# P times v channel-major with v stationary on the two column halves, a normalised P, channel-major gates and an ordered start, in a four-layer hybrid attention kernel

## The chip, the cores and the metric

The kernel runs on one core of a Trainium2 chip. The metric is the device time of one execution in microseconds; a kernel is timed in several runs and the median counts. PE is TensorE, DVE VectorE, ACT ScalarE, POOL GpSimd, SP the queue of SyncE.

## The reference, cut to what matters

There are 256 tokens of 1024 channels, all in fp32. Two "first" layers have three mixers side by side (mLSTM, MoBA with 4 heads, NSA with 4 heads), an output projection and a feed-forward part. Two "second" layers have differential (4 heads), stick-breaking (8 heads) and forgetting attention (8 heads), of which each output is multiplied by a SiLU gate.

```python
def first_block(x, ...):
    for l in range(DEPTH):
        h = rmsnorm(x, norm_mix[l])
        proj = jnp.einsum('bsd,de->bse', h, w_in[l])
        ...                                   # split into m_*, b_*, n_*
        y_m = mlstm(qk[..., :M_WIDTH], qk[..., M_WIDTH:], m_v, m_o, ...)
        y_b = moba(b_q, b_k, b_v, ...)        # here: causal softmax over 256
        y_n = nsa(n_q, n_kc, n_vc, n_ks, n_vs, n_kw, n_vw, n_g, ...)
        mix = jnp.concatenate([y_m, y_b, y_n], axis=-1)
        x = x + jnp.einsum('bse,ed->bsd', mix, w_out[l])
        h = rmsnorm(x, norm_ffn[l])
        u = jnp.square(jax.nn.relu(jnp.einsum('bsd,df->bsf', h, w_ff1[l])))
        x = x + jnp.einsum('bsf,fd->bsd', u, w_ff2[l])
...
# nsa:  gj[:, 0] * o_c + gj[:, 1] * o_s + gj[:, 2] * o_w
def hybrid_layer(x, ...):
    p = rms_norm(x, g_pre) @ w_in
    qa, ka, va, ga, qs, ks, vs, gs, qf, kf, vf, gf, ff = jnp.split(p, split_at, axis=-1)
    ...
    ya = merge(diff_attention(qa, ka, ...)) * jax.nn.silu(ga)
    yb = merge(stick_breaking_attention(qs, ks, vs)) * jax.nn.silu(gs)
    yc = merge(forgetting_attention(qf, kf, vf, cum_log_f)) * jax.nn.silu(gf)
    y = jnp.concatenate([ya, yb, yc], axis=-1) @ w_out
    return x + rms_norm(y, g_post)
```

## The kernel before

**Products with weights.** Each weight unit (for the most part 512 KB) is loaded by SP into one of four raw buffers, and split into a high and a low part in fp32r (`whi` on ACT, line 154; `wlo` on DVE, line 166, and on POOL, line 162, in turns). The activations are split likewise into `xh` and `xl`. A product is three fp32r matmuls (`mm3`, line 262). In `xchunk` the activations are stationary and up to 512 columns of weights move, so the output is token-major (128 tokens x 512 channels). In `wpair` 128 columns of weights are stationary and the 256 tokens move, so the output is channel-major. `rows_all` is the output projection and the second half of the feed-forward part; it takes its left sides from `mix`, channel-major tiles of 256 channels that have been split into `mh` and `ml`, under the keys m, b, n (first layers) and d, s, x (second layers).

**Mixers.** They are written as tasks in two queues ("lanes"), which advance a step at a time between the matmuls of the main stream; a scheduler then sets the order of every engine's instructions. Lane 0 has three PSUM banks, lane 1 two. An attention task of four heads is `att4`: `scores2` makes the scores of two heads at once (64 rows of the array each), DVE masks them, and ACT takes exp with the row sums `den`; `ptr` transposes P in 128 x 128 blocks (line 734); `pv` multiplies a stationary block of the transposed P (128 keys x 128 tokens) by 64 columns of v, three matmuls a head; the token-major output is then multiplied by 1/den on DVE, for NSA by its gates, for s and x by the gates too. `to_mix` transposes it (four per key, line 779) and splits it (ACT line 780, DVE line 781). The diff task scales its P before the transposes (lines 1229, 1230).

**Gates.** Those of s and x come from `xchunk` (token-major, `ev_gate`, line 1385): tanh on ACT, and a DVE instruction at line 1396.

**Start.** SP asks for the first 128 columns of the constants, norm_mix, the four quarters of x with the first weight unit between them, two more units, the other 1568 columns of the constants, and one more unit. POOL's queue asks at once for small rows spread to all partitions (`setup2`, line 370), `cmp_w2`, `diff_lambda` and `m_norm`. Ten bf16 dummy matmuls warm PE (`WARM`); eight transposes of x for each half (`xT`, line 589) come ahead of the first product, of 268 columns.

Of the kernel before, what the change touches and what calls it, by code (L numbers as in the profile page):

```python
# [28 lines left out]
C_CZC = 128  # L29
C_DIF = 512  # L30
C_ML = 896
C_SB = 1152
C_TRI = 1280
C_COS = 1408
C_SIN = 1440
C_CM = 1472
C_CM1 = 1504
C_SUM = 1536
C_KBD = 1552
C_VBD = 1554  # L40
C_S8 = 1558
C_MONE = 1566
C_ONE = 1567
C_DUP = 1568
# [70 lines left out]
class Stream:  # L115
# [16 lines left out]
    def load(self):  # L132
        u = self.n_load
        self.n_load += 1
        a, b, dmas = self.units[u]
        t = self.k.wraw.tile([128, self.SUB], F32, name="raw", tag="raw")
        v = t[:, :a * b].rearrange("p (a b) -> p a b", a=a)
        for f, src in dmas:
            self.k.nc.sync.dma_start(f(v), src)
        self.raw[u] = v, t  # L140
# [42 lines left out]
class K:  # L183
# [132 lines left out]
    def setup(self):  # L316
# [9 lines left out]
        for h in range(2):  # L326
            for tt in range(2):
                sl = slice(h * 512, h * 512 + 512)
                nc.sync.dma_start(self.x[:, tt, sl], A["x"][0, tt * 128:(tt + 1) * 128, sl])
            self.w.load()  # L330
# [15 lines left out]
        self.w.load()  # L346
        nc.sync.dma_start(cp[:, 128:], A["consts"][:, 128:])
        for h in range(2):
            self.bound_half(h, None, False, self.colm, True, "i")
        ps = self.gt()  # L350
        for i in range(self.WARM):
            self.mm(ps, wz[:, :128], wz, True, True)

    def setup2(self):
# [12 lines left out]
        self.rp = {}  # L367
        for name, n in rows:
            self.rp[name] = rp[:, o:o + n].rearrange("p (l c) -> p l c", l=2)
            nc.gpsimd.dma_start(rp[:, o:o + n], dram(A[name], 0, [[0, 128], [1, n]]))  # L370
            o += n
        self.w2 = self.cst.tile([128, 2, 2, 64], F32, name="w2")
        nc.gpsimd.dma_start(self.w2, A["cmp_w2"].rearrange("l w j d -> j l w d"))
# [9 lines left out]
        self.msb = self.cst.tile([128, 128], BF16, name="msb")  # L383
        nc.vector.tensor_copy(self.msb, cp[:, C_SB:C_SB + 128])
        self.s8 = self.cst.tile([128, 8], F32R, name="s8")
        nc.scalar.activation(self.s8, cp[:, C_S8:C_S8 + 8], AF.Copy)
        self.tri = self.cst.tile([128, 129], F32R, name="tri")
        nc.scalar.activation(self.tri[:, 0:128], cp[:, C_TRI:C_TRI + 128], AF.Copy)
        nc.scalar.activation(self.tri[:, 128:129], cp[:, C_MONE:C_MONE + 1], AF.Copy)
# [6 lines left out]
        lt = st[:, 512:1024]  # L396
        nc.gpsimd.dma_start(lt, dram(A["diff_lambda_2"], 0, [[0, 128], [1, 512]]))
        lv = lt.rearrange("p (l a b d) -> p l a b d", l=2, a=2, b=2)
        t = st[:, 1024:1280].rearrange("p (l a d) -> p l a d", l=2, a=2)
# [7 lines left out]
        self.mn = self.cst.tile([128, 512], F32, name="mn")  # L407
# [4 lines left out]
    def plan(self):  # L412
# [41 lines left out]
        for l in range(2):  # L454
# [6 lines left out]
            xch(t, l, W, 3584, 512)  # L461
            xch(t, l, W, 5632, 520)
            for c in range(4096, 5120, 256):
                cols(t, l, W, c, 256, 4)
            xch(t, l, W, 5120, 512)
# [115 lines left out]
    def xT(self, lane, kts, tts, gcol):  # L581
# [5 lines left out]
        for a, kt in enumerate(kts):  # L587
            for b, tt in enumerate(tts):
                i = nc.tensor.transpose(ps[:, a * w + b * 128:a * w + (b + 1) * 128], self.x[:, tt, kt * 128:(kt + 1) * 128],  # L589
                                        self.ident)  # L590
                if nt == 1:
                    self.order(i, "blocks")
# [17 lines left out]
    def bound_half(self, h, acc, scaled, gcol, bcast, flag):  # L610
# [10 lines left out]
        for q in range(2):  # L621
            self.xT(self.lanes[q], (h * 4 + 2 * q, h * 4 + 2 * q + 1), (0, 1), gcol)
# [60 lines left out]
    def ffn(self, l, hold, bound):  # L683
# [17 lines left out]
        def items():  # L701
            m = ff1(0)
            for b in range(16):
# [42 lines left out]
    def att4(self, lane, qf, kf, vf, scale, mask=C_CZC, extra=None, vwait=None):  # L746
# [3 lines left out]
        den = lane.sb("den", 8, bufs=2).rearrange("p (h t) -> p h t", h=4)  # L750
        for h in (0, 2):
            self.scores2(lane, P, nmx, den, h, [(qf(i), kf(i), extra(i) if extra else None) for i in (h, h + 1)], mask, scale)
            yield
# [118 lines left out]
    def nsa_task(self, lane, l, nsA, nq):  # L872
# [48 lines left out]
        o = lane.w().rearrange("p (t h d) -> p t h d", t=2, h=4)  # L921
        for w in range(2):
            ps, rd = yield from self.att4(
                lane, lambda h: qrT[(h % 2) * 64:(h % 2) * 64 + 64, h // 2],
                lambda h: kT[(h % 2) * 64:(h % 2) * 64 + 64, w],
                lambda h, st: nsA[:, st, w * 128 + 64:w * 128 + 128], 0.125)
            gr = lane.sb("gr", 8).rearrange("p (t h) -> p t h", t=2)
            nc.vector.tensor_tensor(gr, gt[:, :, 4 + 4 * w:8 + 4 * w], rd.rearrange("p h t -> p t h"), ALU.mult)
            if w == 0:
                for tt in range(2):  # L930
                    nc.vector.tensor_tensor(o[:, tt], ps[:, tt], gr[:, tt, :, None].to_broadcast([128, 4, 64]), ALU.mult)
            else:
                o2 = lane.w().rearrange("p (t h d) -> p t h d", t=2, h=4)
                for tt in range(2):
                    nc.vector.tensor_tensor(o2[:, tt], ps[:, tt], gr[:, tt, :, None].to_broadcast([128, 4, 64]), ALU.mult)
                nc.gpsimd.tensor_tensor(o, o, o2, ALU.add)
            yield
# [27 lines left out]
        ps = lane.ps()  # L965
        for tt in range(2):
            self.mm(ps[:, tt * 256:(tt + 1) * 256], pc[:64, tt * 128:(tt + 1) * 128],
                    self.vbd.rearrange("p h d -> p (h d)"), True, True)
        o = o.rearrange("p t h d -> p t (h d)")
        nc.vector.tensor_tensor(o, ps.rearrange("p (t c) -> p t c", t=2), o, ALU.add)  # L970
        yield
        yield from self.to_mix(lane, o, ["n%d" % l])

    def moba_task(self, lane, l, qk, bv):
# [29 lines left out]
        ps, rd = yield from self.att4(  # L1004
# [3 lines left out]
        o = lane.w().rearrange("p (t h d) -> p t h d", t=2, h=4)  # L1008
        for tt in range(2):
            nc.vector.tensor_tensor(o[:, tt], ps[:, tt], rd[:, :, tt, None].to_broadcast([128, 4, 64]), ALU.mult)  # L1010
        yield
        yield from self.to_mix(lane, o.rearrange("p t h d -> p t (h d)"), ["b%d" % l])
# [103 lines left out]
    def first_layer(self, l, flag):  # L1116
# [17 lines left out]
        nc.gpsimd.dma_start(self.mn, dram(self.A["m_norm"], l * 512, [[0, 128], [1, 512]]))  # L1134
# [25 lines left out]

        og = self.big.tile([128, 2, 512], F32, name="gate", tag="gate")
# [121 lines left out]
    def sb_task(self, lane, l, half, qkT, vs, gg):  # L1283
# [36 lines left out]
        yield from self.wait("sv%d" % l, "sg%d" % l)  # L1320
        ps = lane.ps().rearrange("p (t h d) -> p t h d", t=2, h=4)
        for i in range(4):
            h = half * 4 + i
            self.pv(ps[:, 0, i], ps[:, 1, i], sp, i, lambda st: vs[:, st, h * 64:h * 64 + 64])
            if i % 2:
                yield
        y = lane.w().rearrange("p (t c) -> p t c", t=2)
# [176 lines left out]
```

## Time and profile before

| what | value |
|---|---|
| median of 3 runs (lowest to highest) | 1140.6 us (1139.28 to 1141.14) |
| the profiled execution's own time | 1142.6 us |
| its span | 1140.8 us |
| mean granted clock of TensorE | 0.994 |
| PE busy | 1101.5 us |
| DVE, ACT, POOL busy | 622.2, 633.6, 552.1 us |
| weights moved | 177.91 MB, 156 GB/s on the mean |

The span is the stretch that the profiler recorded of one execution; the execution's own time has the launch around it. Busy time is the sum over an engine's instructions with overlaps counted once. "Idle before" names who ended a wait.

### The profile page before, as it was taken

What the parts mean: (1) busy time and instruction counts of PE and PEld (TensorE: products, weight loads), DVE (VectorE), ACT (ScalarE), POOL (GpSimd) and SP (SyncE); (2) the same over time, 40 slices, a digit from 0 to 9 for tenths busy, and PEclk for the clock granted to TensorE, in tenths of its full rate; (3) what the DMA queues carried; (4) which work ended last, traced back from release to release, by engine and by line L of the source; (5) the groups of instructions that cost most, each with busy time, mean ns of one, the idle gap of its engine ahead of it and who ended that gap; (6) DMA issues with size and microseconds to landing.
All of it is one profiled execution on the core that took longest, in us unless ns stands there. A gap on an engine that the chain in (4) does not pass through costs nothing.

```text
span 1140.8 us, 18645 instructions
## 1 busy us (share of the span) xinstructions
PE 1101.5 (97%) x6839; PEld 958.6 (84%) x6839; DVE 622.2 (55%) x1319; ACT 633.6 (56%) x1213; POOL 552.1 (48%) x722
## 2 busy tenths in 40 slices
PE   6999999999999999999999999999999999999997
PEld 4788879899998888879999987798997777979886
DVE  3697856333335897675443445572363475633543
ACT  3666546545446656555454445667654366676442
POOL 3854344555554654345555554545542454454521
PEclk9999999999999999999999999999999999999999
DMA  7744244656565643345656555544352535544431
GB/s 209 222 146 130 93 157 148 197 186 193 187 193 156 204 123 101 113 142 171 188 192 191 189 186 164 167 149 149 111 185 92 165 115 185 161 118 136 161 127 39
DMA packets 115515, 177.91 MB, mean 156 GB/s; under 512 B 5808, under 2 KB 75776, under 8 KB 115424
## 3 DMA queue, kind: packets, MB, share of 16 engines
q1 hardware_dynamic: 114368, 174.14, 49.4%
q0 software_dynamic: 832, 2.51, 0.9%
q8 instruction: 53, 0.87, 0.3%
q14 instruction: 38, 0.31, 0.1%
q10 hardware_dynamic: 224, 0.08, 0.0%
HBM read 175.66 MB, written 1.05 MB: 155 GB/s over the span
## 4 chain that ended last, share of the span: by engine, by line
PE 76%; DVE 5%; ACT 2%; issue 1%; DMA 0%; POOL 0%; DVEq 0%; ACTq 0%; POOLq 0%
PE g L256 44%; PE a L256 29%; ACT whi L154 1%; PE a L734 1%; DVE wlo L166 1%; PE a L589 1%; PE a L779 1%; DVE P L1229 1%; DVE den L1226 0%; DMA raw<-in_w_in_dram 0%; DVE x L655 0%; PE a L1273 0%; ACT w L1246 0%; ACT P L299 0%; DVE P L1230 0%
## 5 line engine op out<-in xcount | busy, mean ns | idle before, releaser
L162 POOL TENSOR_TENSOR wlo<-raw,whi 128x256 fp32r<-128x256 f32 (+1 forms) x652 | 508.7, 812 | 524.5 <-ACT whi L154 476.7
L154 ACT ACTIVATE whi<-raw 128x1024 fp32r<-128x1024 f32 (+2 forms) x328 | 345.0, 1054 | 328.0 <-PE a L256 165.7
L166 DVE TENSOR_TENSOR wlo<-raw,whi 128x1024 fp32r<-128x1024 f32 (+2 forms) x164 | 214.5, 1308 | 216.5 <-ACT whi L154 215.5
L256 PE MATMUL g<-wlo,xh 128*128 128x512 f32 (+3 forms) x480 | 176.4, 368 | 1.2 <-POOL wlo L162 1.0
L256 PE MATMUL g<-whi,xh 128*128 128x512 f32 (+3 forms) x480 | 173.8, 368 | 0.0
L256 PE MATMUL g<-whi,xl 128*128 128x512 f32 (+3 forms) x480 | 173.7, 365 | 0.0
L256 PE MATMUL a<-xl,whi 128*128 128x256 f32 x512 | 143.6, 281 | 1.5 <-DVE xl L598 1.5
L256 PE MATMUL a<-xh,wlo 128*128 128x256 f32 x512 | 143.4, 280 | 0.0
L256 PE MATMUL a<-xh,whi 128*128 128x256 f32 x512 | 143.3, 280 | 0.0
L256 PE MATMUL g<-whi,mh 128*128 128x512 f32 x312 | 123.5, 396 | 3.6 <-ACT mh L780 3.6
L256 PE MATMUL g<-wlo,mh 128*128 128x512 f32 x312 | 123.6, 396 | 0.0
L256 PE MATMUL g<-whi,ml 128*128 128x512 f32 x312 | 118.7, 393 | 0.0
L256 PE MATMUL g<-xh,whi 128*128 128x256 f32 x400 | 114.1, 285 | 1.9 <-DVE qkT L1432 1.9
L256 PE MATMUL g<-xh,wlo 128*128 128x256 f32 x400 | 114.5, 286 | 0.7 <-DVE wlo L166 0.7
L256 PE MATMUL g<-xl,whi 128*128 128x256 f32 x400 | 114.9, 287 | 0.0
L256 PEld LDWEIGHTS g<-wlo,xh 128*128 128x128 f32 x480 | 92.2, 192 | 17.7 <-issue 2.7
L256 PEld LDWEIGHTS g<-whi,xh 128*128 128x128 f32 x480 | 91.5, 192 | 14.4 <-issue 1.5
L256 PEld LDWEIGHTS g<-whi,xl 128*128 128x128 f32 x480 | 92.0, 192 | 13.4 <-issue 1.0
L256 PEld LDWEIGHTS a<-xl,whi 128*128 128x128 f32 x512 | 96.1, 188 | 3.0 <-DVE xl L598 1.7
L256 PEld LDWEIGHTS a<-xh,whi 128*128 128x128 f32 x512 | 96.1, 188 | 1.3
L256 PEld LDWEIGHTS a<-xh,wlo 128*128 128x128 f32 x512 | 96.4, 188 | 0.0
L256 PEld LDWEIGHTS g<-xh,whi 128*128 128x128 f32 x400 | 75.3, 188 | 3.2 <-DVE qkT L1432 2.4
(332 smaller groups left out, 1776.7 us busy)
## 6 DMA issues: line engine op xcount, KB each, us to landing
raw<-in_w_in_dram SPq DMA_DIRECT2D x130, 512.0 KB, 3.9
raw<-in_w_ff_dram SPq DMA_DIRECT2D x128, 512.0 KB, 4.0
raw<-in_w_out_dram SPq DMA_DIRECT2D x40, 512.0 KB, 3.4
raw<-in_w_in_dram SPq DMA_DIRECT2D x16, 520.0 KB, 4.3
raw<-in_cmp_w_dram SPq DMA_DIRECT2D x16, 256.0 KB, 3.8
raw<-in_w_in_dram SPq DMA_DIRECT2D x4, 268.0 KB, 12.9
raw<-in_w_in_dram SPq DMA_DIRECT2D x2, 536.0 KB, 4.3
x<-in_x_dram SPq DMA_DIRECT2D x4, 256.0 KB, 9.7
```

The lines of the kernel that those rows point to most:

```text
L154: nc.scalar.activation(hv, v, AF.Copy)
L162: nc.gpsimd.tensor_tensor(lo[:, c:d], raw[:, c:d], hi[:, c:d].bitcast(F32), ALU.subtract)
L166: nc.vector.tensor_tensor(lv, v, hv.bitcast(F32), ALU.subtract)
L256: i = self.nc.tensor.matmul(out, l, r, start=st, stop=sp, skip_group_check=skip)
L589: i = nc.tensor.transpose(ps[:, a * w + b * 128:a * w + (b + 1) * 128], self.x[:, tt, kt * 128:(kt + 1) * 128], self.ident)
L734: nc.tensor.transpose(ps[:, b * 128:(b + 1) * 128], P[:, i, b * 128:(b + 1) * 128], self.ident)
L779: nc.tensor.transpose(ps[:, (j * 2 + tt) * 128:(j * 2 + tt + 1) * 128], y[:, tt, c:c + 128], self.ident)
L1229: nc.vector.tensor_scalar(P[:, 2 * i + 1, a:b], P[:, 2 * i + 1, a:b], den[:, 2 * i + 1, tt:tt + 1], None, ALU.mult)
```

## The change

**P times v.** `pvT` takes the place of `pv`: v (128 keys x 64 channels) is stationary on columns 0 to 63 for one head and 64 to 127 for the other, P transposed moves (256 tokens for the first block of keys, 128 for the second), and the output is channel-major. `att4` takes the reciprocal of `den` per pair of heads and scales P itself on DVE before the transposes; for NSA the gate is in that factor, and the two attention parts and the compressed part are summed in one PSUM bank of lane 0. `split_mix` splits the channel-major output with no transposes, for the keys b, n, s and x; m and d stay with `to_mix`.

**Gates.** Those of s and x are made by `wpair` (`gateT`), channel-major; x's gates are now the last chunk ahead of the output projection, and v with the forget columns the first of that mixer (before: gates with the forget columns first, v last).

**Start.** The constants are laid out anew and loaded in three parts: on SP 128 columns first and, behind x and four weight units, 288 and 640; on POOL the last 640. The rows of the first layers are asked for behind a POOL copy of x's last column. The rows of the second layers and `diff_lambda` are written in `setup3`, in the first feed-forward part. Ten and then four dummy matmuls stand ahead of the two halves' transposes, in this order.

```diff
+    def pvT(self, ps, PT, i, v, first=True, last=True):
+        out = ps[:, (i // 2) * 256:(i // 2) * 256 + 256]
+        for a, c in ((0, slice(0, 256)), (1, slice(256, 384))):
+            for j in range(2):
+                self.mm(out[j * 64:j * 64 + 64, a * 128:256], v(i + j, a), PT[:, i + j, c], first and i == 0 and a == 0,
+                        last and i == 2 and a == 1, skip=True)
...
         for h in (0, 2):
             self.scores2(lane, P, nmx, den, h, [...], mask, scale)
-            yield
-            yield
-        rd = lane.sb("rd", 8, bufs=2).rearrange("p (h t) -> p h t", h=4)
-        nc.vector.reciprocal(rd, den)
+            nc.vector.reciprocal(rd[:, h:h + 2], den[:, h:h + 2])
+            if gate is not None:
+                nc.vector.tensor_tensor(rd[:, h:h + 2], rd[:, h:h + 2], gate[...], ALU.mult)
+            for i in (h, h + 1):
+                for tt, (a, b) in enumerate(((0, 128), (128, 384))):
+                    nc.vector.tensor_scalar(P[:, i, a:b], P[:, i, a:b], rd[:, i, tt:tt + 1], None, ALU.mult)
+            yield
+            yield
...
-        ps = lane.ps().rearrange("p (t h d) -> p t h d", t=2, h=4)
-        for h in range(4):
-            self.pv(ps[:, 0, h], ps[:, 1, h], P, h, lambda st: vf(h, st))
-            if h % 2 == 1:
-                yield
-        return ps, rd
+        ps = lane.ps() if acc is None else acc
+        for h in (0, 2):
+            self.pvT(ps, P, h, vf, acc is None, last)
+            yield
+        return ps
+
+    def split_mix(self, lane, src, key):
...
+        nc.scalar.activation(h, src, AF.Copy)
+        nc.vector.tensor_tensor(l, src, h.bitcast(F32), ALU.subtract)
...
+        def gateT():
+            g = self.big.tile([128, 4, 256], F32, name="gate", tag="gate")
+            for j in (0, 2):
+                gs = self.gt2()
+                self.wpair(gs)
+                for i in range(2):
+                    nc.vector.scalar_tensor_tensor(g[:, j + i], gs[i], 0.5, rb[:, 0], ALU.mult, ALU.mult)
...
+            self.act(t, f, AF.Tanh)
+            nc.vector.scalar_tensor_tensor(f, t, 1.0, f, ALU.add, ALU.mult)
...
-        self.xchunk(512, ev_gate(gg), both=True)
+        gates["s"] = gateT()
...
-        self.w.load()
-        nc.sync.dma_start(cp[:, 128:], A["consts"][:, 128:])
+        for _ in range(3):
+            self.w.load("boot")
+        for a, b in ((C_COS, C_CZC), (C_CZC, C_DIF)):
+            self.order(nc.sync.dma_start(cp[:, a:b], A["consts"][:, a:b]), "boot")
...
+        self.order(nc.gpsimd.tensor_copy(rp[:, 0:1], self.x[:, 1, DM - 1:DM]), "rows")
```

The order of POOL's instructions at the start, before (`rp` are the small rows, `cp` the constants, `wlo` the first weight's low part):

```order
L370 DMA rp<-in_moba_qk_norm_dram 128x256
L370 DMA rp<-in_nsa_q_norm_dram 128x128
L370 DMA rp<-in_nsa_k_norm_dram 128x384
L370 DMA rp<-in_b_if_dram 128x16
L370 DMA rp<-in_forget_bias_dram 128x16
L370 DMA rp<-in_diff_subln_dram 128x256
L373 DMA w_194<-in_cmp_w_dram 128x4x64
...
L397 DMA qkT<-in_diff_lambda_dram 128x512
L1134 DMA mn<-in_m_norm_dram 128x512
...
L162 TENSOR_TENSOR wlo<-raw,whi 128x256
```

And of the changed kernel:

```order
L1190 DMA mn<-in_m_norm_dram 128x512
...
L407 DMA cp<-in_consts_dram 128x640
L409 DMA rp<-in_forget_bias_dram 128x16
L409 DMA rp<-in_diff_subln_dram 128x256
L375 COPY rp<-x 128x1
L382 DMA rp<-in_moba_qk_norm_dram 128x256
L382 DMA rp<-in_nsa_q_norm_dram 128x128
L382 DMA rp<-in_nsa_k_norm_dram 128x384
L382 DMA rp<-in_b_if_dram 128x16
L384 DMA w_195<-in_cmp_w_dram 128x4x64
...
L164 TENSOR_TENSOR wlo<-raw,whi 128x256
```

Six of the loads now stand behind the copy of x, or later; `m_norm`, the last constants, forget_bias and diff_subln stand ahead of it.

PE in the first layer 0, where NSA's first P times v stands, before (`nsA` holds its v, `P_676` is P transposed):

```order
L256 MATMUL g<-whi,xh 128x512
L256 MATMUL a_862<-nsA,P_676 128x64 x9
L256 MATMUL a_960<-kT,qkT 128x128
L256 MATMUL a_862<-nsA,P_676 128x64 x3
L256 MATMUL a_961<-kT,qkT 128x128
```

And after, its second pair of heads:

```order
L258 MATMUL g<-xh,whi 128x256
L258 MATMUL a_862<-P_664,nsA 64x256
L258 MATMUL a_916<-kT,qkT 128x128
L258 MATMUL a_916<-kT,qkT 128x256
L258 MATMUL g<-xl,whi 128x256
L258 MATMUL a_862<-P_664,nsA 64x256
L258 MATMUL a_862<-P_664,nsA 64x128 x2
L258 MATMUL a_917<-kT,qkT 128x128
```

The two heads' matmuls of 256 tokens (`64x256`) have other matmuls between them here, and the two of 128 tokens are together.

PE at the last P times v of the kernel (forgetting attention of layer 1), before, where it stands within the output projection (`mh`, `ml`):

```order
L256 MATMUL a_11583<-v,P_11383 128x64 x2
L256 MATMUL g<-whi,mh 128x512
L256 MATMUL g<-wlo,mh 128x512
L256 MATMUL a_11583<-v,P_11383 128x64 x4
L256 MATMUL g<-whi,ml 128x512
L256 MATMUL g<-whi,mh 128x512
L256 MATMUL g<-wlo,mh 128x512
L256 MATMUL a_11583<-v,P_11383 128x64 x3
L734 MATMUL a_11489<-cp,P_11402 128x128 x3
L256 MATMUL a_11583<-v,P_11383 128x64 x3
L256 MATMUL g<-whi,ml 128x512
```

And after, where it stands within the gates' chunk (`xh`, `xl`), ahead of the output projection:

```order
L258 MATMUL a_11719<-P_11487,v 64x256 x2
L258 MATMUL a_11719<-P_11487,v 64x128 x2
...
L258 MATMUL g<-xh,whi 128x256
L258 MATMUL a_11724<-P_11512,v 64x256 x2
L258 MATMUL a_11724<-P_11512,v 64x128 x2
L258 MATMUL a_11724<-P_11512,v 64x256 x2
L258 MATMUL a_11724<-P_11512,v 64x128 x2
L258 MATMUL g<-xl,whi 128x256
```

## Rows read from the trace of the kernel before

**Rows 1.** The page: busy time, share of the span, instructions; the chain's share by engine:

```profile
PE 1101.5 (97%) x6839; PEld 958.6 (84%) x6839; DVE 622.2 (55%) x1319; ACT 633.6 (56%) x1213; POOL 552.1 (48%) x722
...
PE 76%; DVE 5%; ACT 2%; issue 1%; DMA 0%; POOL 0%; DVEq 0%; ACTq 0%; POOLq 0%
```

**Rows 2.** PE's waits: line, releaser; us in total, times, longest:

```profile
PE a L589 <- DMA x<-in_x_dram: 9.4, 4, 4.1
PE g L256 <- ACT mh L780: 3.6, 3, 1.2
...
PE a L734 <- DVE P L1230: 0.4, 2, 0.2
```

**Rows 3.** The chain that ended last, two stretches of the main stream: start us, us:

```profile
820.95 12.81 PE g L256 x108
...
923.48 12.42 PE g L256 x53
```

**Rows 4.** PE by form, P times v: busy, mean ns of one | idle before:

```profile
L256 PE MATMUL a<-v,P 128*128 128x64 f32 x240 | 29.4, 269 | 0.0
...
L256 PE MATMUL a<-nsA,P 128*128 128x64 f32 x96 | 11.8, 273 | 0.0
```

**Rows 5.** PE's timeline round one group of P times v: start us, us:

```profile
889.89 0.39 PE L256 MATMUL a<-wlo,mh 128*128 128x512 f32 x1
890.12 2.79 PE L256 MATMUL a<-v,P 128*128 128x64 f32 x24
...
893.04 0.39 PE L256 MATMUL g<-whi,mh 128*128 128x512 f32 x1
```

**Rows 6.** PE's timeline round three transposes of P:

```profile
860.88 0.39 PE L256 MATMUL g<-whi,xl 128*128 128x512 f32 x1
861.11 0.49 PE L734 MATMUL a<-cp,P 128*128 128x128 f32 x3
...
861.92 0.39 PE L256 MATMUL g<-whi,xl 128*128 128x512 f32 x1
```

**Rows 7.** PE's timeline round a group of scores of stationary 64 rows:

```profile
729.53 0.40 PE L256 MATMUL g<-whi,xh 128*128 128x512 f32 x1
729.86 2.23 PE L256 MATMUL a<-qkT 64*128 64x128 f32 x20
732.02 0.50 PE L256 MATMUL g<-wlo,xh 128*128 128x512 f32 x1
732.36 0.39 PE L256 MATMUL g<-whi,xl 128*128 128x512 f32 x1
```

**Rows 8.** PE's timeline where stationary tiles of 64 columns end:

```profile
384.86 0.28 PE L256 MATMUL g<-wlo,y 128*64 128x256 f32 x1
384.98 0.41 PE L256 MATMUL g<-whi,xh 128*128 128x264 f32 x2
```

**Rows 9.** DVE by form: scaling of the diff task's P, reciprocal of den:

```profile
L1229 DVE TENSOR_SCALAR P<-P,den 128x256 f32<-128x256 f32 x8 | 3.7, 466 | 0.0
...
L1229 DVE TENSOR_SCALAR P<-P,den 128x128 f32<-128x128 f32 x8 | 3.3, 417 | 0.0
...
L756 DVE RECIPROCAL rd<-den 128x8 f32<-128x8 f32 x10 | 2.0, 198 | 5.2 <-ACT P L299 5.1
```

**Rows 10.** The windows of 20 us: busy (x instructions) by engine, PEclk, DMA share:

```profile
80.00:100.00 20.00, 20.00 (x127) 16.55 (x126) 19.44 (x49) 11.36 (x29) 12.72 (x15) 1.00 0.29 81
...
420.00:440.00 20.00, 18.74 (x98) 14.43 (x96) 16.89 (x46) 9.86 (x24) 8.67 (x14) 0.91 0.36 105
```

**Rows 11.** PE's timeline at the start, the transposes of x:

```profile
15.23 0.69 PE L589 MATMUL a<-cp,x 128*128 128x128 f32 x2 [4.13 <-DMA x<-in_x_dram]
18.33 1.54 PE L589 MATMUL a<-cp,x 128*128 128x128 f32 x6 [2.41 <-DMA x<-in_x_dram]
```

**Rows 12.** DMA in the first 20 us: a queue, and one issue's landing:

```profile
q0 software_dynamic: 464, 1.20, 33.4%
...
mn<-in_m_norm_dram POOLq DMA_DIRECT2D x1, 256.0 KB, 11.4
```

More of the change, by code (lines that the diff above doesn't have):

```diff
@@ L28 @@
 C_ID = 0
[L29 to L44, printed above, removed]
+C_COS = 128
+C_SIN = 160
+C_CM = 192
+C_CM1 = 224
+C_SUM = 256
+C_KBD = 272
+C_VBD = 274
+C_S8 = 278
+C_MONE = 286
+C_ONE = 287
+C_DUP = 288
+C_CZC = 416
+C_ML = 800
+C_DIF = 1056
+C_SB = 1440
+C_TRI = 1568
 C_N = 1696
@@ L345, in setup @@
         self.rb = self.cst.tile([128, 2, 256], F32, name="rb")
-        self.w.load()
-        nc.sync.dma_start(cp[:, 128:], A["consts"][:, 128:])
-        for h in range(2):
-            self.bound_half(h, None, False, self.colm, True, "i")
         ps = self.gt()
-        for i in range(self.WARM):
-            self.mm(ps, wz[:, :128], wz, True, True)
+        for n, h in zip((self.WARM, 4), range(2)):
+            for i in range(n):
+                self.order(nc.tensor.matmul(ps, wz[:, :128], wz, start=True, stop=True), "warm")
+            self.bound_half(h, None, False, self.colm, True, "i", "warm")
     def setup2(self):
@@ L919, in nsa_task @@
         nc.vector.reciprocal(gt, gt)
-        o = lane.w().rearrange("p (t h d) -> p t h d", t=2, h=4)
+        acc = None
         for w in range(2):
-            ps, rd = yield from self.att4(
+            acc = yield from self.att4(
                 lane, lambda h: qrT[(h % 2) * 64:(h % 2) * 64 + 64, h // 2],
                 lambda h: kT[(h % 2) * 64:(h % 2) * 64 + 64, w],
[L926 to L936, printed above, removed]
-            yield
+                lambda h, st: nsA[:, st, w * 128 + 64:w * 128 + 128], 0.125, acc=acc, last=False,
+                gate=gt[:, :, 4 + 4 * w:8 + 4 * w])
         yield from self.wait("cmp%d" % l)
@@ L964, in nsa_task @@
         yield
[L965 to L970, printed above, removed]
+        for a in range(2):
+            self.mm(acc[:, a * 256:(a + 1) * 256], self.vbd[:, 2 * a:2 * a + 2].rearrange("p h d -> p (h d)"), pc[:64], False, a == 1,
+                    skip=True)
         yield
-        yield from self.to_mix(lane, o, ["n%d" % l])
+        self.split_mix(lane, acc, "n%d" % l)
     def moba_task(self, lane, l, qk, bv):
@@ L1281, in diff_prep, with sb_task @@
         self.done.add("dqk%d" % l)
-    def sb_task(self, lane, l, half, qkT, vs, gg):
+    def sb_task(self, lane, l, half, qkT, vs, gates):
         nc = self.nc
@@ L1319, in sb_task @@
                 yield
[L1320 to L1327, printed above, removed]
-        for tt in range(2):
-            nc.vector.scalar_tensor_tensor(y[:, tt], ps[:, tt].rearrange("p h d -> p (h d)"), self.rsh[:, tt:tt + 1],
-                                           gg[:, tt, half * 256:half * 256 + 256], ALU.mult, ALU.mult)
-        yield
-        yield from self.to_mix(lane, y, ["s%d%d" % (l, half)])
+        yield from self.wait("sv%d" % l)
+        ps = lane.ps()
+        for i in (0, 2):
+            self.pvT(ps, sp, i, lambda h, st: vs[:, st, (half * 4 + h) * 64:(half * 4 + h) * 64 + 64])
+            yield
+        yield from self.wait("sg%d" % l)
+        y = lane.w()
+        nc.vector.tensor_tensor(y, ps, gates["s"][:, 2 * half:2 * half + 2].rearrange("p a t -> p (a t)"), ALU.mult)
+        self.split_mix(lane, y, "s%d%d" % (l, half))
     def fgate_task(self, lane, l, ff):
@@ L1353, in fgate_task, with fox_task @@
         self.done.add("fg%d" % l)
-    def fox_task(self, lane, l, half, qkT, vf, gg):
+    def fox_task(self, lane, l, half, qkT, vf, gates):
         nc = self.nc
```

143 lines of the change are left out of this document (82 added, 61 removed).

## The prediction

> **What bounds the kernel now.** I read the page first: TensorE (PE) is busy 97% of the span, and the chain of work that ended last lies on it for 76%, against 5% on VectorE (DVE) [rows 1]. So time is gained where PE's own work shrinks, or where one of its waits goes; work that leaves DVE, ScalarE or GpSimd gives nothing by itself. Then PE's waits: the largest is the start, 9.4 us for the four loads of x; next 3.6 us for the split of the mixed heads (line 780); and only 0.4 us for the diff task's P, which is already scaled on DVE before it is transposed [rows 2]. The rest of the span is PE content, and the chain prices its two common forms: 108 matmuls of 256 columns in 12.81 us, 0.1186 each, and 53 of 512 columns in 12.42 us, 0.2343 each [rows 3].
>
> **P times v, today.** Its records are 240 + 96 = 336 [rows 4]; a matmul of fp32 data leaves two records, so these are 168 matmuls. The mean duration in those rows (269 ns) is pipelined and is not what one costs. The timeline gives that: from the 512-column matmul at 889.89 to the one at 893.04 are 3.15 us, which hold 24 such records and two 512-column matmuls (2 x 0.234), so (3.15 - 0.47)/24 = 0.112 us a record [rows 5], and 336 x 0.112 = 37.6 us in all. A record with 64 columns moving costs as much as one with 128: three P transposes (128 moving) between 860.88 and 861.92 take 1.04 less three 512-column matmuls (0.70) = 0.34, or 0.112 each [rows 6].
>
> **P times v, changed.** With v stationary, the two heads of a pair use the two column halves of the array: 56 matmuls of 256 columns and 56 of 128, two records each. No 256-column fp32 record of this form is in the trace; twice the 128-column one is 0.22. One after the other this is 112 x 0.22 + 112 x 0.112 = 37.2 us: nothing gained. Side by side it would be half, 18.6. Whether column halves run side by side no row of before shows. The nearest rows are the scores, where two heads use the two row halves: 20 records stand between 729.53 and 732.36, less a 512-column matmul on either end 2.36 us; that is two pairs and one single head, each of two 128- and two 256-column records [rows 7]. Singly they would be five times 2 x (0.112 + 0.22) = 3.3 us; as three slots they are 2.0. So row halves do run side by side, at about 0.4 us extra for the group. I take overlap for column halves as well, since each half has its own weights and its own output partitions. But the order of the changed program sets other PE work between the halves of 11 of the 28 pairs of 256 columns and of two pairs of 128 (as at P_664 in the rows of the changed order), which then run singly: 11 x 0.44 + 2 x 0.22 = 5.3 us given back. Content: 18.6 + 5.3 = 23.9, against 37.6: -13.7.
>
> Entering and leaving the half-array form: bound from above by the 0.4 us of a scores group, from below by nothing, as the matmuls with 64 stationary columns show, which pass to full ones at the same 0.12 pitch (384.86, 384.98) [rows 8]. The new groups are 34. I stand nearer to the second rows, which are the same column form, and take 0.02 each: **-13** in all (-13.7 to -0.1 with 0.4 a group).
>
> The Trainium skill, "TensorEngine Tiling (Array Packing)", Key Properties, says two things of this: that tiles operate independently, and that changing the tiling mode drains the engine. The first agrees with rows 7 and would give the -13; the second agrees with the 0.4 us of rows 7 but not with rows 8, and by it alone the 34 groups would cost some 13.6 us (an estimate from rows 7 and the count).
>
> **The other parts on PE.** The transposes to channels are dropped for 12 keys (b, n, s, x), 4 each: 48 x 0.112 = **-5.4**. The gates of s and x become channel-major: 384 matmuls of 256 columns (45.5 us) for 192 of 512 (45.0): **+0.6** (up to +2, as 256-column stretches also run a little slower than 0.1186). The transposes of the two m groups of a first layer stand together in the changed order, where 22 outproj matmuls stood between them; of the waits of line 780 (3 times, 3.6 us [rows 2]) that may save one, **-1**.
>
> **What DVE and the others take over.** Per pair of heads there is a reciprocal (0.20) and four scalings of P, two of 0.417 and two of 0.466: 1.97 us [rows 9], and for 20 pairs 39 us. They stand between the last exp and P's first transpose, where only one reciprocal of four heads stood. What hides them is the main stream: PE has hundreds of 256- or 512-column matmuls to put between a task's scores and its transposes, 53 of them in the first layer's nsa part where one stood. The diff task has the same chain now and costs PE 0.4 us [rows 2]. What it costs if the cover is gone: 2 us a pair. DVE is full where the first layer's tasks meet (19.44 of 20 us at 80 to 100) [rows 10], so some of it is late there. Bounds: nothing, and 6 us (three pairs); I take **+1.5**. The scaling after the product (36 instructions on DVE of these sizes, and a sum on POOL) goes, off PE's path. The channel-major output is split straight from PSUM, one hop less before outproj; outproj takes keys d first, then s, then x, so the last keys are wanted late and I count nothing. The nsa sum now holds a PSUM bank of lane 0 through the compress part: its scores have two banks left, which they use as a pair; a wait there is inside the +1.5.
>
> **The start.** The transposes of x wait for its four loads, the last until 18.33 [rows 11], since on the DMA engines x shares the time with the rows that POOL asks for: in the first 20 us its queue moved 1.20 MB at 33.4% of the engines' time, and m_norm took 11.4 us to land [rows 12]. Now the requests of moba_qk_norm, nsa norms, b_if and cmp_w2 stand behind a copy of x's last column, so they start after x; diff_lambda (256 KB) goes much later. But m_norm (256 KB), 320 KB of consts, forget_bias and diff_subln (136 KB) stand ahead of that copy in POOL's order: about 0.71 MB of 1.17 stays early. By bytes, 39% of that queue's third of the engines goes, 0.13 x 18 = 2.4 us; all of its third would be 6. What goes are mostly rows spread to all partitions in small packets, which hold an engine longer than their bytes say, so I take 4.3, between the two. Against that POOL issues five requests after x has landed and before its first wlo, and the first chunk needs that wlo; no row prices a request on POOL, so I put 0.8 back for the five, with nothing and 2 as its ends. **-3.5**, from 0 to -8. Four dummy matmuls more stand between x's halves; they cost at most 4 x 0.47 = 1.9 (half clock), while PE waits anyway. Nothing is gained at all if DVE's casts of the early consts (they stand in front of the first xl in DVE's order) wait for a load that lands as late as m_norm does, 11.4 us after its request.
>
> **The sum.** -13 - 5.4 + 0.6 - 1 + 1.5 - 3.5 = **-20.8**. The profiled execution's own time is 1142.6 (span 1140.8 and 1.8 around it), 2.0 above the median of the runs, 1140.6. So 1121.8 for a profile and **1120** for the median.
>
> **Rivals.**
> (a) Column halves don't overlap: they feed 128 rows each, where the scores' halves share the rows. P times v then gains 0.4 instead of 13: 1132.5. For it: no row shows two column halves at work. Against: rows 7, a form of half array that overlaps. 0.17.
> (b) They overlap, but each of the 34 groups pays the 0.4 us of a scores group: 13 more, 1133. For it: rows 7. Against: rows 8. 0.13.
> (c) The other side: scaling P on DVE ahead of the transposes stalls PE. 39 us are put into that chain, and to be slower it must give back 20.8 + 2.3. A wait also lowers the clock after it: between 420 and 440 PE has 1.3 us idle and a granted clock of 0.91, which loses another 1.8 of the 20 [rows 10]. At 2 + 1.8 us a pair it decides from 6 of the 20 pairs on that are fully exposed (from 12 on, if the clock holds); at 10 pairs the time is 1120 + 38 - 1.5 = 1156. For it: DVE at 19.44 of 20. Against: 0.4 us in the diff task, and DVE's 55% mean. 0.07.
> (d) The start moves nothing, as the early consts and m_norm load POOL's queue and DVE's casts: 1123.5. 0.13.
> The rest, 0.5, is the forecast.
>
> **Range and chances.** Below: the start's whole -8, no stall and no price of the 34 groups, 1120 - 4.5 - 1.5 - 0.7 = 1113, and 1112 with a second m wait less. Upward it takes in (a) and (b) with a stall or two: 1136. What is left out is (c), and (a) or (b) with more stalls. A measurement here tells 0.2%, 2.3 us. (a), (b) and (d) are all faster than that. So faster 0.87; same 0.06, the shallow end of (c) beside (a) or (b); slower 0.07.
>
> **What will show it.** P times v: the two halves' records starting a few ns apart, and a group of 8 records of a pair taking 0.66 us rather than 1.33; if not, (a). After such a group the next 512-column matmul at 0.23 or later: (b). PE's waits naming DVE P or den at the transposes: (c). The x waits' sum below 6 us and the first 268-column matmul before 16 us: the start; if it is at 19, (d). PE's busy time should be near 1084. The prediction is wrong if the time is above 1136 or below 1112, and its reason is wrong if the 13 us of P times v aren't there though the total fits.

## The result, and the profile after

The changed kernel takes 1123.17 us (median of 4 runs, 1120.8 to 1125.21) beside 1139.94 us of the kernel before: a ratio of 0.9848, 95% interval 0.9835 to 0.986, or 17.3 us less by that ratio. Run again beside other runs of before it came to 0.9865 (0.985 to 0.9881), 15.4 us less. The forecast was 1120, or 20.8 less. Its profiled execution took 1120.8 us (span 1119.0), the lowest of its runs; that of the second time had a span of 1122.1 and the same pattern.

The page of the changed kernel, the lines that answer to [rows 1]:

```profile
PE 1083.5 (97%) x6875; PEld 937.4 (84%) x6875; DVE 647.8 (58%) x1393; ACT 631.7 (56%) x1207; POOL 564.6 (50%) x722
...
PE 75%; DVE 6%; ACT 2%; issue 1%; POOL 0%; DMA 0%; DVEq 0%; ACTq 0%; POOLq 0%
```

PE's busy time fell by 18.0 us to what the forecast named (1084), and DVE took on 26 us. PE's waits (line, releaser; us in total, times, longest), beside [rows 2]:

```profile
PE a L610 <- DMA x<-in_x_dram: 5.0, 2, 4.5
PE a L826 <- DVE w L1141: 3.3, 1, 3.3
PE a L258 <- DVE w L625: 2.7, 1, 2.7
...
PE g L258 <- ACT mh L827: 0.8, 1, 0.8
PE a L258 <- DVE P L761: 0.8, 2, 0.5
...
PE a L757 <- DVE P L791: 0.5, 1, 0.5
```

The wait for x is down from 9.4 to 5.0 us and that for the split of the m keys from 3.6 to 0.8. New are 3.3 us for an mLSTM output that DVE makes (line 1141), ahead of transposes in the second first layer, and 2.7 us for the norm's factor at the start. The scaled P (line 791) is waited for once, 0.5 us, and the copy of its transposes (line 761) twice, 0.8 us.

P times v, with PE's timeline round one group in the forgetting attention, beside [rows 5]:

```profile
856.11 0.28 PE L258 MATMUL g<-xh,wlo 128*128 128x256 f32 x1
856.32 0.87 PE L258 MATMUL a<-P,v 128*64 128x256 f32 x8
857.12 0.39 PE L258 MATMUL g<-xh,whi 128*128 128x256 f32 x1
857.34 0.28 PE L258 MATMUL g<-xl,whi 128*128 128x256 f32 x1
```

Eight records, four of 256 and four of 128 columns, stand in 0.80 us (856.32 to 857.12); singly, at the 0.22 and 0.112 us of the prediction, they would take 1.33. The column halves do run side by side. But the group is dear to enter and to leave: from 856.11 to 857.34 are 1.23 us, less two 256-column matmuls of 0.119 that is 0.99, where the content is 0.66. The 0.33 us lie ahead of the first record (0.21 after a matmul of 0.12), in the first record, ahead of the first full matmul, and behind it (0.22 instead of 0.12).

The same sum over the whole trace, of the time from one PE record's start to the next, by kind (worked out from the records of the three executions; us). What passes ahead of a group counts here for the record before it:

```
kind                                 before   changed (2nd time)   merged run
P times v, diff included               46.9       37.4              30.0
matmuls of 64 rows (scores and such)   53.1       45.6              44.6
transposes, waits between them in      59.6       47.1              41.5
main stream (all fp32r with weights)  946.1      951.0             957.6
all other                              26.8       32.8              32.2
```

The first three kinds take 29.5 us less in the second column, the other two 10.9 more. Part of the 10.9 has only moved: 4.8 us of it stand behind the dummy matmuls, where the wait for x falls now, and the entries of P times v, 3.8 us more than before, count in the main for the matmuls ahead of them. With the entry ahead of a group counted for the group, P times v (diff left out) goes from 37.7 to 32.2 us, and with the dearer first matmul behind it from 39.5 to 35.2. The second kind stood in no term of the prediction. The 64-row groups are 62 before and 51 after, at 59.8 and 51.0 us with their entry. Most of that, some 6 us, is in the forgetting mixer. PE's timeline there before, two heads of a pair:

```profile
852.50 0.92 PE L256 MATMUL a<-qkT 64*128 64x128 f32 x4
853.07 0.52 PE L256 MATMUL a<-cumr,s 64*128 64x384 f32 x1
853.52 0.50 PE L256 MATMUL g<-whi,xh 128*128 128x512 f32 x1
853.95 0.92 PE L256 MATMUL a<-qkT 64*128 64x128 f32 x4
854.52 0.52 PE L256 MATMUL a<-cumr,s 64*128 64x384 f32 x1
854.98 0.50 PE L256 MATMUL g<-wlo,xh 128*128 128x512 f32 x1
```

And after:

```profile
842.54 0.28 PE L258 MATMUL g<-xl,whi 128*128 128x256 f32 x1
842.75 0.93 PE L258 MATMUL a<-qkT 64*128 64x128 f32 x8
843.32 0.53 PE L258 MATMUL a<-cumr,s 64*128 64x384 f32 x2
843.78 0.39 PE L258 MATMUL g<-xh,wlo 128*128 128x256 f32 x1
```

Before, one head alone holds PE for 1.02 us and then its partner as long again, with a main matmul between; after, both take 1.03 together. Before, six of the eight heads stood alone in the first of the two layers, and four in the second; after, none.

### The profile page after: what moved, and what is told of

It reads as the page before. It is cut to its first block, busy times and chain, and to the rows that moved or that the text cites. A ratio compares the mean times of both kernels' runs of the same rounds, so it can differ in the third digit from the quotient of the medians.

```text
span 1119.0 us, 18807 instructions
## 1 busy us (share of the span) xinstructions
PE 1083.5 (97%) x6875; PEld 937.4 (84%) x6875; DVE 647.8 (58%) x1393; ACT 631.7 (56%) x1207; POOL 564.6 (50%) x722
## 4 chain that ended last, share of the span: by engine, by line
PE 75%; DVE 6%; ACT 2%; issue 1%; POOL 0%; DMA 0%; DVEq 0%; ACTq 0%; POOLq 0%
PE g L258 44%; PE a L258 29%; ACT whi L156 1%; DVE wlo L168 1%; PE a L757 1%; DVE P L1259 1%; PE a L610 1%; DVE den L1256 0%; DMA raw<-in_w_in_dram 0%; POOL y L1019 0%; PE a L1303 0%; ACT w L1276 0%; DVE P L791 0%; DVE P L1260 0%; DVE x L639 0%
## 5 line engine op out<-in xcount | busy, mean ns | idle before, releaser
L164 POOL TENSOR_TENSOR wlo<-raw,whi 128x256 fp32r<-128x256 f32 (+1 forms) x652 | 523.6, 835 | 475.1 <-ACT whi L156 422.2
L258 PE MATMUL g<-xh,whi 128*128 128x256 f32 x528 | 151.0, 286 | 2.0 <-DVE qkT L1462 2.0
L258 PE MATMUL g<-xl,whi 128*128 128x256 f32 x528 | 152.0, 288 | 0.0
L258 PE MATMUL g<-wlo,xh 128*128 128x512 f32 (+3 forms) x416 | 149.9, 361 | 1.3 <-POOL wlo L164 1.2
L258 PE MATMUL g<-xh,wlo 128*128 128x256 f32 x528 | 151.0, 286 | 0.0
L258 PE MATMUL g<-whi,xl 128*128 128x512 f32 (+3 forms) x416 | 148.8, 362 | 1.1 <-DVE xl L619 1.1
L258 PE MATMUL g<-whi,xh 128*128 128x512 f32 (+3 forms) x416 | 147.8, 361 | 0.0
L258 PEld LDWEIGHTS g<-xh,whi 128*128 128x128 f32 x528 | 99.4, 188 | 5.4 <-issue 2.9
L258 PEld LDWEIGHTS g<-xl,whi 128*128 128x128 f32 x528 | 99.5, 188 | 3.9 <-issue 3.6
L258 PEld LDWEIGHTS g<-xh,wlo 128*128 128x128 f32 x528 | 99.6, 189 | 3.6 <-issue 3.5
```

Source lines behind the costliest of these rows:

```text
L164: nc.gpsimd.tensor_tensor(lo[:, c:d], raw[:, c:d], hi[:, c:d].bitcast(F32), ALU.subtract)
L258: i = self.nc.tensor.matmul(out, l, r, start=st, stop=sp, skip_group_check=skip)
```

## The experiments

Ratios are to the kernel before in the same group of runs.

**The four heads in one piece** (e1_merged, on the changed kernel). The head that is ready last is issued first, and a chain of order holds the others behind it.

```diff
...
-            for j in range(2):
-                self.mm(out[...], v(i + j, a), PT[:, i + j, c], first and i == 0 and a == 0, last and i == 2 and a == 1, skip=True)
+            for j in (1, 0):
+                k = self.nc.tensor.matmul(out[...], v(i + j, a), PT[:, i + j, c], start=first and i == 2 and a == 0, stop=last and i == 0 and a == 1, ...)
+                self.order(k, "pv%d" % self.npv)
...
-        for h in (0, 2):
+        for h in (2, 0):
             self.pvT(ps, P, h, vf, acc is None, last)
-            yield
+        yield
...                                           # the same for the stick-breaking task
```

> The changed kernel, with the products of all four heads of a task issued in one piece, the heads that are ready last first: 13 groups instead of 34, and no half that runs singly. Theory A (column halves overlap, but every group pays about 0.24 to 0.34 us to enter and leave the half-array form, as the changed kernel's trace shows): a group of 16 records takes 1.54 us there, so 14 x 1.54 = 21.6 us for what takes 32 us now: about 10 us faster than the changed kernel, 1113 us. Theory B (groups cost nothing, only halves that run singly do): 5.4 us faster, 1118. Theory C (the later product holds up its lane, or lateness shows up as waits): no gain, 1123 or more.

Measured: 1113.72 us, ratio 0.9755 (0.9737 to 0.9774); again 0.9763 (0.9745 to 0.9781). That is 10 to 12 us less than the changed kernel: theory A. PE's timeline round one of its 13 groups:

```profile
1015.15 0.28 PE L258 MATMUL g<-wlo,xh 128*128 128x256 f32 x1
1015.36 1.52 PE L775 MATMUL a<-P,v 128*64 128x256 f32 x16
1016.81 0.39 PE L258 MATMUL g<-whi,xl 128*128 128x256 f32 x1
1017.04 0.40 PE L258 MATMUL g<-whi,xh 128*128 128x256 f32 x2
```

Sixteen records pay the entry that eight paid: 1.89 less 0.24 is 1.65, for a content of 1.32. So it is the number of groups and of halves left alone that makes the product's price: with entry and the matmul behind, the product takes 26.0 us here and 35.2 in the changed kernel. Two of the groups still wait for the copy of the transposed P:

```profile
PE a L775 <- DVE P L761: 3.4, 2, 1.7
```

**Head after head** (e2_serial).

```diff
-        for a, c in ((0, slice(0, 256)), (1, slice(256, 384))):
-            for j in range(2):
+        for j in range(2):
+            for a, c in ((0, slice(0, 256)), (1, slice(256, 384))):
```

> The changed kernel, with the product of one head issued whole before that of the next, so that records of the two column halves meet only where one head ends and the next begins. 39 groups instead of 34. Theory A (overlap of neighbours is what makes the product cheap): 28 pairs go from about 0.65 us to 1.2 us, less what already ran singly, plus 5 groups of 0.3 us: 10 to 12 us slower than the changed kernel, 1134. Rival (the halves' overlap is worth little, since the product isn't what PE waits on): within 3 us of the changed kernel.

Measured: 1129.19 us, 0.9893 (0.9879 to 0.9906), 3 to 5 us slower than the changed kernel: between the two. The edit did not do what it was made for. Its timeline at the last group:

```profile
1086.17 1.57 PE L258 MATMUL a<-P,v 128*64 128x256 f32 x16
1087.67 0.39 PE L258 MATMUL g<-xl,whi 128*128 128x256 f32 x1
```

Sixteen records in 1.50 us, as if they had been issued in pairs. In the raw records the second head's first one starts 13 ns after the first head's (1086.173 and 1086.186), while the first head's matmul of 128 columns, which was issued ahead of it, starts only at 1086.656. P times v took 4.7 us more in the trace, in 39 groups for 34; that the groups and the halves whose partner stands in another one are what it costs agrees with the first run, but isn't shown apart. So this run says nothing on what overlap is worth.

**The start of before** (e3_start: setup, setup2 and the place of m_norm as in the kernel before; e6_merged_start: the same on the merged run).

```diff
-        for _ in range(3):
-            self.w.load("boot")
-        for a, b in ((C_COS, C_CZC), (C_CZC, C_DIF)):
-            self.order(nc.sync.dma_start(cp[:, a:b], A["consts"][:, a:b]), "boot")
+        self.w.load()
+        nc.sync.dma_start(cp[:, 128:], A["consts"][:, 128:])
...
-        self.order(nc.gpsimd.tensor_copy(rp[:, 0:1], self.x[:, 1, DM - 1:DM]), "rows")
```

> The changed kernel with the start of the kernel before: order of loads, POOL's requests, dummy matmuls and constants in one piece. Theory A (the start is worth what the milestones show where the compress part begins, 3.6 us): 1126.5. Rival (its whole 5.3 us at the first product are kept): 1128.5. Rival (the start is worth nothing, since what is gained is lost again before the first attention task): 1123.

> The run with merged products, with the start of the kernel before. Theory A (the start is worth the 3 to 4 us that the milestones of the profiled executions show at the compress part): 3 to 4 us slower than the merged run, 0.9785 of the kernel before. Theory B (it is worth nothing, as the first comparison had it at 0.0005 of the kernel before): 0.9755 to 0.977.

Measured: 1124.3 us, 0.9853 (0.9836 to 0.9871), and 1113.19 us, 0.977 (0.9754 to 0.9786), beside 0.9848 and 0.9865 for the changed kernel and 0.9755 and 0.9763 for the merged one. So the new start is worth 1.7 us at most, within the uncertainty of these runs. Yet the first product does begin earlier in the profiled execution. PE's timeline of the changed kernel, beside [rows 11]:

```profile
11.87 0.47 PE L610 MATMUL a<-cp,x 128*128 128x128 f32 x1 [4.55 <-DMA x<-in_x_dram]
12.79 1.76 PE L610 MATMUL a<-cp,x 128*128 128x128 f32 x7 [0.45 <-DMA x<-in_x_dram]
14.20 0.80 PE L258 MATMUL g<-whi,xh 128*128 128x268 f32 x2
...
20.37 0.49 PE L258 MATMUL a<-w,cp 128*128 128x128 f32 x2 [2.69 <-DVE w L625]
```

The product starts at 14.20 instead of 19.52. Its matmuls of 268 columns then stand 0.22 us apart (granted clock 0.50 at 12 to 16 us, the lower level of 1.2 GHz, after the wait of 4.55 us), as they do before (20.11 to 23.91), and PE waits once more at 20.37. At the compress part (the first matmul of `cmph`) 4.1 us of the 5.3 are left: 62.73 beside 66.81. That lead is not lost later: against the profiled execution of e3_start, whose product starts at 19.95, the changed kernel is 4.6 us ahead at the compress part and 4.5 at 350 us.

But the start of before is not always as late as in these two. In the other two profiled executions that have it, the product starts at 17.27 (e6_merged_start) and at 15.69 (e9_scaled, below), and the compress part at 63.13 and 63.16. In the ten with the new start the product starts at 13.73 to 14.65 and the compress part at 62.73 to 65.79. So the new start makes the arrival of x steady; beside an early execution of the old one it gains nothing at the compress part.

**More dummy matmuls** (e11_warm, on the merged run, with that run again as e12_merged_again).

```diff
-        for n, h in zip((self.WARM, 4), range(2)):
+        for n, h in zip((self.WARM, 20), range(2)):
```

> The run with merged products, with 20 dummy matmuls instead of 4 ahead of the second half of x, so that PE works on through the 4.6 us in which it waits for x. Theory A (the idle stretch is what lowers the clock of the first product, whose 268-column matmuls then stand 0.22 us apart instead of 0.12): the first chunks are 2 to 4 us faster, 1110 to 1112 us. Rival (the first product is bound by the low parts and the norm's chain on DVE, not by PE): within 1 us of the merged run.

> The run with merged products again, as the base for the run with more dummy matmuls: 0.9755 of the kernel before, by its first comparison.

Measured: 1114.66 us, 0.9777 (0.9758 to 0.9795), beside 0.9763: no gain. PE's timeline shows why:

```profile
6.55 4.48 PE L356 MATMUL g<-wz 128*128 128x512 bf16 x20
...
15.66 0.29 PE L258 MATMUL g<-whi,xl 128*128 128x268 f32 x1
15.78 0.41 PE L258 MATMUL g<-whi,xh 128*128 128x268 f32 x2
22.51 0.58 PE L258 MATMUL g<-xh,whi 128*128 128x256 f32 x1 [6.32 <-ACT whi L156]
```

The granted clock is 1.00 there, 2.4 GHz, and the 268-column matmuls stand 0.12 us apart. But then PE waits 6.32 us for the high part of a weight unit (and the granted clock is 0.50 again at 20 to 24 us), and ACT in its turn waits for loads; its waits in the first 30 us of this run:

```profile
ACT whi L156 <- DMA raw<-in_w_in_dram: 9.3, 5, 3.2
```

With x early and the clock up, what bounds the start in this run is the arrival of the weights behind x.

**P not scaled** (e4_noscale) and **P scaled alone** (e9_scaled, on the kernel before).

```diff
 e4_noscale, on the changed kernel
-                    nc.vector.tensor_scalar(P[:, i, a:b], P[:, i, a:b], rd[:, i, tt:tt + 1], None, ALU.mult)
 e9_scaled, on the kernel before, after each pair's scores
+            nc.vector.reciprocal(rd[:, h:h + 2], den[:, h:h + 2])
+            for i in (h, h + 1):
+                for tt, (a, b) in enumerate(((0, 128), (128, 384))):
+                    nc.vector.tensor_scalar(P[:, i, a:b], P[:, i, a:b], rd[:, i, tt:tt + 1], None, ALU.mult)
```

> The changed kernel without the 80 scalings of P on DVE (the softmax stays undivided; this part of the computation is left out), the reciprocals stay. Theory A (they are covered by the main stream): up to 1.5 us faster, 1121.5 to 1123. Rival (DVE's chain ahead of the transposes is what ate the missing gain): 5 us faster or more, 1118 or less.

> The kernel before with one part of the change alone: a reciprocal per pair of heads and the scaling of P on DVE ahead of its transposes (the scaling of the output is left in, so this part is done twice). Theory A (the chain is covered, as the changed kernel without it showed): within 2 us of the kernel before. Rival (the scalings are what spaces the scores so that two heads stand together, worth some of the 9 us by which the scores' groups fell): 3 us faster or more. Rival (c) of the prediction (they stall PE): 4 us slower or more.

The first kernel leaves out the division of the softmax; the second divides twice. Measured: without the scalings 1123.32 us, 0.9843 (0.9829 to 0.9856), the changed kernel's own time. But its scores fell apart again in part (59 groups of 64 rows, 55.5 us, for 51 and 51.0), so this run took two things away that may offset each other. In the kernel before the scalings alone cost 1.0067 (1.005 to 1.0084), 6 to 10 us: rival (c)'s mechanism, at a third of the price from which it decides. Its largest new wait is not at P's transposes but further on:

```profile
PE a L783 <- DVE w L1115: 5.1, 2, 2.8
```

This is the mLSTM output; the changed kernel has the same wait at line 826, 3.3 us. The scalings alone bring it about in the kernel before, which has none there, but they are not its whole cause: without them 2.5 us of the 3.3 stay in the changed kernel, and in the 10 us ahead of the wait DVE has no scaling there, only the mLSTM's own chain and the low parts of weights. The scores stayed apart (60 groups, 60.9 us), so the scalings alone don't pair them.

**Gates token-major, chunks in the old order** (e5_gates).

```diff
-        gates["s"] = gateT()
+        self.xchunk(512, ev_gate(gg), both=True)
...
-        self.xchunk(520, ev_vf, pieces=[(0, 264), (264, 256)], both=True)
+        self.xchunk(520, ev_gate(gg, ff), pieces=[(0, 264), (264, 256)], both=True)
...
-        gates["x"] = gateT()
+        self.xchunk(512, ev_to(v))
```

> The changed kernel with the gates of s and x token-major as before, and the chunks of the forgetting mixer in the order of before (gates with the forget columns, q and k, v last). The gates then stand in the wrong layout, so this part of the computation is changed. Theory A (the forecast: the gates' new form costs 0.6 us and the order nothing): 0.6 us faster than the changed kernel. Theory B (the order of the chunks is what set the forgetting mixer's scores in pairs: 9 of its 10-record groups take 1.12 us in the changed kernel where before most heads stood alone at 1.11 us each, 6 us in all): 5 us slower, if its scores fall apart again; in the order of this kernel about half of them do, so 2 to 3 us slower.

This kernel leaves the gates in the wrong layout for the product behind them, at the same size. Measured: 1122.74 us, 0.9846 (0.9828 to 0.9863), beside 0.9865 in the same group: 2 us faster, with an uncertainty as large. Theory B falls: the 64-row groups take 51.4 us here too, and the forgetting mixer's heads still stand in pairs.

**Scores in one piece** (e8_scores, on the merged run: the two heads' matmuls in a chain of order, the second head first).

```diff
-            for p, (q, k, _) in zip(ps, heads):
-                self.mm(p[:, a:b], q[:, c], k[:, 0:b - a], st or a == 0, st, skip=not st)
+            for p, (q, k, _) in list(zip(ps, heads))[::-1]:
+                m = self.nc.tensor.matmul(p[:, a:b], q[:, c], k[:, 0:b - a], start=st or a == 0, stop=st, ...)
+                self.order(m, "sc%d" % self.nsc)
```

> The run with merged products, and the scores of a pair of heads in one piece as well, the head whose bank is free last first. Theory A (a half that stands alone costs as much as a pair, and each group its entry): the scores of NSA and MoBA lose some 4 us of single halves in two layers, less what their later start costs: 2 to 4 us faster than the merged run. Rival (the scores' cost in the main stream is set by the banks' release, so waiting for the second bank costs what pairing gives): within 1 us of it.

Measured: 1113.88 us, 0.9785 (0.9766 to 0.9803): no faster than the merged run. The groups were 51 instead of 48, at 49.5 and 49.6 us; the chain didn't bring them together.

**Transposes put back** (e10_transposes) and the changed kernel again (e7_after).

```diff
+        ps = lane.ps()
+        for j in range(4):
+            nc.tensor.transpose(ps[:, j * 128:(j + 1) * 128], self.x[:, 0, j * 128:(j + 1) * 128], self.ident)
         nc.scalar.activation(h, src, AF.Copy)
```

> The changed kernel with four unused transposes of x into a bank of the lane at each of the 12 splits, as many as the change removed. Theory A (each costs PE its 0.112 us and nothing else): 5.4 us slower than the changed kernel, 0.9900 to 0.9912 of the kernel before. Rival (they cost more, since they take a PSUM bank of the lane too, so their removal gave more than I summed): 8 us slower or more. Rival (less, since they stand in gaps): under 3 us.

> The changed kernel again, as the base of this group of runs: 0.985 of the kernel before, by its first comparison.

Measured: 0.9906 (0.989 to 0.9922), beside 0.9848 and 0.9865: 5 to 7 us slower, theory A. The changed kernel itself came to 0.9865.

## Why the prediction was right, and where its terms were not

The time lay in the range, 3 us above the forecast, but by luck. The prediction said that its reason is wrong if the 13 us of P times v aren't there though the total fits, and that is what happened: 5.5 were there, and a gain of 8.8 us that stood in no term made up for the rest.

- **P times v, -13: mis-sized.** It measured -5.5 with the entry (37.7 us to 32.2), and -4.3 with the matmul behind as well. Overlap was as forecast. What failed is the price of entering and leaving: I took 0.02 us a group and it is 0.33, near the 0.4 of the scores that I kept as the bound, so rival (b) had the right mechanism. The step that failed is the reading of [rows 8] as the same form: those matmuls have 64 stationary columns and pass to full ones free of charge, and the new groups don't. It is not the partner that makes the difference: nine of the 34 groups hold one matmul on one half alone, and they cost 0.28 to 0.34 us beside their content too. The Trainium skill, "TensorEngine Tiling (Array Packing)", Key Properties, has it that a change of tiling mode drains the TensorE; the 34 groups agree, rows 8 don't. The matmuls of rows 8 move fp32r data, like the main stream, and those of P times v plain fp32; but two transposes of plain fp32 with 64 stationary columns pass free as well (125.47 to 126.15 in the changed kernel). So what a block of 64 columns must have to pay is left open. Merging the groups gave back 10 to 12 us.

  One half alone in the changed kernel, where the two records of 128 columns take 0.37 us (content 0.22) and the full matmul behind them 0.22 instead of 0.12:

```profile
1073.54 0.43 PE L258 MATMUL a<-P,v 128*64 128x128 f32 x2
1073.91 0.39 PE L258 MATMUL g<-xl,whi 128*128 128x256 f32 x1
1074.13 0.28 PE L258 MATMUL g<-xh,wlo 128*128 128x256 f32 x1
```

  The trace of before had a nearer row than rows 8: four records of the compress part, plain fp32 with 32 and 64 stationary columns and no partner. They come 0.21 us after the full matmul ahead, and the full one behind takes 0.23, where 0.12 is the pitch:

```profile
66.60 0.28 PE L256 MATMUL g<-whi,xl 128*128 128x256 f32 x1
66.81 0.56 PE L256 MATMUL a<-w,cmph 128*32 128x64 f32 x4
67.30 0.39 PE L256 MATMUL g<-whi,xh 128*128 128x264 f32 x1
67.53 0.28 PE L256 MATMUL g<-wlo,xh 128*128 128x264 f32 x1
```

- **Transposes, -5.4: right.** Put back they cost 5 to 7 us.
- **Gates, +0.6, up to +2: near.** Undone, with their order, 2 us less, uncertain by as much.
- **Start, -3.5: wrong in what is left of it.** x came earlier by 5.3 us at the first product (4.3 were forecast), and its waits were 5.0 us, below the 6 named; both signs of the start were there, but the runs show 1.7 us at most. The step that failed is that the wait of 9.4 us, read from one execution, was taken for every execution's: the product of the old start begins anywhere from 15.69 to 19.95 us. And an earlier x is not the kernel's gain in full: in the run with more dummy matmuls PE waits for the weights behind it. How often the old start is late four profiled executions don't tell. Nor are the packets small that were to hold the engines longer than their bytes say: the 464 of that queue hold 1.20 MB [rows 12], 2.6 KB each, beside 1.3 KB in the queue of x (2363 packets, 3.14 MB at 49.3%); per byte they do hold the engines longer, and why is open.
- **m keys, -1: -2.8 in the profile**, and 3.3 us given back at line 826.
- **DVE, +1.5: the right size at the place named, and another wait beside it.** P's transposes and products wait 1.3 us. The 3.3 us are at the mLSTM output, of which 2.5 stay without the scalings. In the old kernel the same scalings cost 6 to 10 us, so rival (c) was no idle one; why the changed kernel bears them isn't shown, as the run without them lost pairs of scores too.
- **Not in the sum: the 64-row groups, -8.8 us in the trace.** They made up for P times v. No single part that I undid or made alone explains it: without the scalings half of it is lost (55.5 us), alone they don't give it (60.9), and the gates' old order keeps it (51.4). The forgetting mixer's heads stand in pairs without the scalings and with the gates' old order, and not with the scalings alone, so neither of the two pairs them there; which of the other parts does, or whether it is the scheduler's placing of the whole, is left open. A wait of 2.5 us at the border of the two second layers (before, at 911.38) went as well. It stands in the kernel before with scalings too (2.51 us at 915.08); the lower clock that followed it in before didn't follow there.

The best kernel found is the merged one, 0.9755 and 0.9763 of the kernel before, about 27 us less.

## What to carry to other kernels

Half-array products in a full-array stream are paid by the group: count the groups in the order that comes out, and let the operand that is ready last go first, so that what belongs together stands together. A price from a row holds for the form of that row: before it is carried over, look for every row that is near, and see if they agree. A load that comes earlier gives little if the next one in the queue is needed right after it: ask what is late next, and look at more than one execution before a wait for a load is priced. And where a scheduler sets the order, an edit to one task moves the others; compare all kinds of work on the bound engine, not the edited one alone.

## What the runs showed of the hardware

A matmul on the free column half started 13 ns after the first one (1086.173 and 1086.186), ahead of one for the other half that was issued earlier (1086.656). Sixteen records of four heads took 1.45 us. Between full matmuls a group on the column halves cost 0.33 us beside its content, whether it had 8 records or 16; one half alone cost 0.28 to 0.34. Blocks of 64 stationary columns of fp32r, in a stream of fp32r, cost no such entry [rows 8], nor did two transposes of fp32 with 64 stationary columns. The wait for the same four loads of x put the first product at 15.69 to 19.95 us in four executions of one order of requests.
